# A casting DMA instead of a rounding on ScalarE: the weights' high part straight from DRAM

## The chip, the cores and the metric

The kernel runs on one core of a Trainium2 chip. It is one program for five engines that run side by side and wait for each other by semaphores: TensorE (PE, matrix products), VectorE (DVE), ScalarE (ACT), GpSimd (POOL) and SyncE (SP). DMA transfers are issued by SyncE, GpSimd and ScalarE, each from its own queue in order. The metric is the device time of one execution in microseconds. The median before is 1366.24 us of 3 runs (1365.65 to 1368.66).

## The reference

One layer of a decoder, for a prompt of 1024 tokens and for 8 decode tokens:

```python
h = _rmsnorm(x, norm1_g)
proj = h @ w_in                                   # 1024 x 2304
pool_out = pool_mixer(proj[..., :512])            # windows 2, 4, 8, 16
rwkv_out = rwkv7_mixer(proj[..., 512:])           # 8 heads of 64, state update
x = x + concat(pool_out, rwkv_out) @ w_out        # 1024 x 1024
h2 = _rmsnorm(x, norm2_g)
x = x + square(relu(h2 @ w_up)) @ w_down          # 1024 x 4096, 4096 x 1024
y = _rmsnorm(x, norm_f_g)
```

All inputs are float32. The large products (w_in, w_out, w_up, w_down) are computed in three parts: a float32 operand is split into a high part, rounded to the format fp32r, and a low part, the rest of the subtraction. High times high, high times low and low times high are added up in PSUM.

## The kernel before

The tokens stand in columns, 1032 of them, and a product is computed in blocks of up to 512 columns: blocks of 256 (one of 264) for w_in, and the three blocks BLK of 512, 260 and 260 columns in the MLP. A weight tile `[P, 512]` holds four 128 x 128 weights. For w_in and w_up a row of outputs takes two tiles, for w_down one (four of the 32 hidden tiles at a time).

`weights(src)` brings a tile. It loads the raw float32 tile `wr` (4 buffers, NWR) by a DMA of GpSimd's queue (line 155 or 157), ScalarE rounds it into the high part `wh` (by `act`, line 92; the call is on line 164), and VectorE subtracts to get the low part `wl` (line 165). `wh` and `wl` have 6 buffers each (NWH). So a raw tile waits for the subtract of the tile four back, a high part for the last matmul that reads the tile six back. `gemm` issues the matmuls (line 175), three for each weight, the one with the low weight last.

The stages: at the start the tokens are loaded and split (`token_block`); then the mixer, twice, once for each half of the prompt (`ORDER` gives the sequence of its steps). `R` steps are projections, `S` and `I` prepare a unit of two heads (the inverse of its triangular blocks goes through DRAM: `blk<-AA` on line 464, `Dg<-blk` on line 467, and then line 512, all on SyncE's queue), and `C` is the chain over time. The output projection follows, first for 512 columns, then, with `opb`, for 520. Then the MLP: 32 up tiles `ups_of(f)` (their PSUM pool has four buffers), and eight groups of eight down tiles `down(g, m, b, w)`. In groups 0 to 6 the order is four ups, eight downs. A down block goes into the PSUM pool `psd`, which has two buffers, and VectorE adds it to the residual `x` (line 949); these lines of `down` and its loop are not in the listing below:

```python
ps_d = open_pool(ctx, "psd", 2, space=PSUM)
def down(g, m, b, w):
    ps = ps_d.tile([P, 512], F32, tag="d", name=f"dn{g}_{m}_{b}")
    gemm(ps[:, :n], w, [...])
    V.tensor_tensor(d, ps[:, :n], d, op=ALU.add)
for m in range(KT):
    w = weights(I["w_down"][g, m])
    for b in range(3):
        down(g, m, b, w)
```

The order of each engine's instructions is set when the program is built, by a scheduler that goes by priorities (in the order of the code, moved by `tc.high_priority`) and its own costs. On the chip each engine works through its queue in that order: an instruction that waits holds up those behind it.

Of the kernel before, what the change touches and what calls it, by code (L numbers as in the profile page):

```python
# [15 lines left out]
P = 128  # L16
# [68 lines left out]
def _build(ctx, nc, tc, I, O, dbg):  # L85
    V, A, PE, SY, GP = nc.vector, nc.scalar, nc.tensor, nc.sync, nc.gpsimd

    def f32(ap):
        return ap.bitcast(F32)

    def act(out, in_, func=AF.Copy, bias=0.0, scale=1.0, **k):
        A.activation(out, in_, func, bias=bias, scale=scale, **k)  # L92
# [54 lines left out]
    def weights(src, into=None):  # L147

        out = []
        n = int(np.prod(src.shape[1:]))  # L150
        for o in range(0, n, 512):
            w = min(512, n - o)
            raw = wp.tile([P, 512], F32, tag="wr", name="wr", bufs=NWR)
            if len(src.shape) > 2:
                GP.dma_start(raw.rearrange("p (m c) -> p m c", c=P), src)
            else:
                GP.dma_start(raw[:, :w], src[:, o:o + w])
            if into:
                h, l = into
            else:  # L160
                h = wp.tile([P, 512], F32R, tag="wh", name="wh", bufs=NWH)
                l = wp.tile([P, 512], F32R, tag="wl", name="wl", bufs=NWH)
            with tc.high_priority(offset=LEADW):
                act(h[:, :w], raw[:, :w])
                V.tensor_tensor(l[:, :w], raw[:, :w], f32(h[:, :w]), op=ALU.subtract)  # L165
            out += [(h[:, c:c + P], l[:, c:c + P]) for c in range(0, w, P)]
        return out
# [96 lines left out]
    def project(m, half, use):  # L264
        w = ahead.pop(m, None) or weights(I["w_in"][m])
        for b in (2 * half, 2 * half + 1):
            if b in late:
                with tc.high_priority(offset=LEADX):
                    next(late.pop(b))
            project_block(m, w, b, use)  # L270
# [442 lines left out]
    def pool_group(g, half):  # L713
# [8 lines left out]
        def use(b, n, ps, rs):  # L722
            l0 = 16 + 256 * (b % 2)
            V.tensor_tensor(u[:, l0:l0 + n], ps[:, :n], rs[:, :n], op=ALU.mult)

        w = weights(I["w_in"][g])
        for i in range(2):
            project_block(g, w, 2 * half + i, use)
# [45 lines left out]

    starts = [token_block(b) for b in range(2)]
    ahead[16] = weights(I["w_in"][16, :, 0:512])
    next(starts[0])
    ahead[16] += weights(I["w_in"][16, :, 512:])
# [7 lines left out]
    for w, r, src in ((wup, R[0], "w_lora_up"), (aup, R[1], "a_lora_up")):  # L786
        raw = wp.tile([P, 512], F32, tag="wr", name=f"r{src}", bufs=NWR)
# [128 lines left out]
    with tc.tile_pool(name="opb", bufs=1, reuse_waits="tile") as op:  # L916
        ops = [mixed(op, k, 1, 3) for k in range(KT - 1)]
        for m in range(KT):
            w = weights(I["w_out"][m, :, :(KT - 1) * P])
# [12 lines left out]
    w = weights(I["w_up"][0])  # L932
# [20 lines left out]
    for g in range(7):  # L953
        ups_of(4 * g + 4)
        for m in range(KT):
            w = weights(I["w_down"][g, m])
# [111 lines left out]
```

## Time and profile before

| | before |
|---|---|
| median of 3 runs | 1366.24 us |
| profiled execution | 1369.13 us |
| its span | 1367.4 us |
| TensorE busy | 1306.5 us (96%) |
| VectorE busy | 829.6 us (61%) |
| ScalarE busy | 592.7 us (43%), of these 143.8 in 230 roundings of 512 columns |
| GpSimd busy | 156.5 us (11%) |
| DMA traffic | 94.82 MB, 66.04 of them by GpSimd's queue |
| mean granted TensorE clock | 0.987 |

The span is the time from the first to the last instruction. Matmuls are pipelined and their ends are modelled, so two matmuls overlap in the trace, and TensorE's busy time is not the time that it needs. A wait is put down to what came last. The chain of work that ended last is followed back from the last instruction: at each step to what released it, or to the instruction before it on its engine.

### The profile page before, as it was taken

The numbers are of one execution on the slowest core, as the hardware profiler recorded it, in microseconds if no ns is written. First come the engines' busy times: TensorE is split into PE (matmuls) and PEld (weight loads), VectorE is DVE, ScalarE is ACT, GpSimd is POOL, SyncE is SP. The second block draws the span as 40 slices with busy tenths as digits, with TensorE's granted clock in tenths as the row PEclk, the third lists the DMA queues.
The fourth block names the chain that finished last, engine by engine and source line by source line (L and its number), as shares of the span: only waits on it lengthen the run. The fifth ranks groups of instructions, "written<-read, shape, count | busy, mean of one in ns | idle before, by whom it ended". The sixth has DMA issues, their size and how long they took to land.

```text
span 1367.4 us, 24591 instructions
## 1 busy us (share of the span) xinstructions
PE 1306.5 (96%) x9844; PEld 1158.8 (85%) x9844; DVE 829.6 (61%) x1832; ACT 592.7 (43%) x1466; POOL 156.5 (11%) x306
## 2 busy tenths in 40 slices
PE   5999999999999999999999999999999999999996
PEld 5987778788777777798999999999999999999986
DVE  8887677778778656748644435445444354453447
ACT  7768777877777758526211212112111121121123
POOL 4101000210010021120010100100000100000000
PEclk9999999899999989999999999999999999999998
DMA  6323123222221244531111111111111111111103
GB/s 199 97 55 89 39 47 83 100 96 54 59 63 42 67 152 147 167 125 59 47 54 39 55 47 39 55 40 47 55 40 54 47 46 48 45 48 48 47 7 124
DMA packets 75315, 94.82 MB, mean 69 GB/s; under 512 B 46168, under 2 KB 52440, under 8 KB 75192
## 3 DMA queue, kind: packets, MB, share of 16 engines
q0 software_dynamic: 20480, 66.04, 15.1%
q1 hardware_dynamic: 53392, 25.36, 7.1%
q10 hardware_dynamic: 1328, 1.85, 0.4%
q8 instruction: 77, 1.26, 0.4%
q14 instruction: 38, 0.31, 0.1%
HBM read 79.67 MB, written 13.78 MB: 68 GB/s over the span
## 4 chain that ended last, share of the span: by engine, by line
PE 75%; ACT 9%; DVE 9%; DMA 3%; issue 2%; POOL 1%; SPq 0%; DVEq 0%; POOLq 0%; ACTq 0%
PE dn L175 26%; PE up L175 26%; PE pj L175 7%; PE mx L175 5%; ACT SV L92 2%; DVE tm L496 1%; PE sc L403 1%; PE pcs L580 1%; ACT Es L92 1%; ACT TT L92 1%; PE pcs L577 1%; DVE SV L589 1%; ACT wh L92 1%; PE pcs L573 1%; PE bkt L417 1%
## 5 line engine op out<-in xcount | busy, mean ns | idle before, releaser
L92 ACT ACTIVATE wh<-wr 128x512 fp32r<-128x512 f32 x230 | 143.8, 626 | 353.4 <-PE dn L175 276.2
L175 PE MATMUL up<-h2h,wl 128*128 128x260 f32 (+1 forms) x768 | 245.8, 320 | 0.0
L175 PE MATMUL up<-h2h,wh 128*128 128x260 f32 (+1 forms) x768 | 245.2, 320 | 0.5 <-DVE u L910 0.5
L175 PE MATMUL up<-h2l,wh 128*128 128x260 f32 (+1 forms) x768 | 245.0, 320 | 0.0
L175 PE MATMUL dn<-uh,wl 128*128 128x512 f32 (+1 forms) x720 | 231.2, 321 | 0.0
L175 PE MATMUL dn<-ul,wh 128*128 128x512 f32 (+1 forms) x720 | 230.8, 321 | 0.0
L175 PE MATMUL dn<-uh,wh 128*128 128x512 f32 (+1 forms) x720 | 230.5, 320 | 0.0
L949 DVE TENSOR_TENSOR x<-dn,x 128x260 f32<-128x260 f32 (+1 forms) x192 | 99.1, 516 | 189.8 <-PE dn L175 189.8
L175 PE MATMUL pj<-xh,wh 128*128 128x256 f32 (+1 forms) x576 | 175.3, 304 | 13.9 <-ACT wh L92 13.7
L165 DVE TENSOR_TENSOR wl<-wr,wh 128x512 fp32r<-128x512 f32 x230 | 156.5, 684 | 44.6 <-ACT wh L92 37.8
L175 PE MATMUL pj<-xh,wl 128*128 128x256 f32 (+1 forms) x576 | 171.0, 297 | 0.2 <-DVE wl L165 0.2
L175 PE MATMUL pj<-xl,wh 128*128 128x256 f32 (+1 forms) x576 | 170.5, 296 | 0.0
L175 PEld LDWEIGHTS up<-h2l,wh 128*128 128x128 f32 x768 | 144.6, 188 | 12.1 <-DVE h2l L892 0.4
L175 PEld LDWEIGHTS up<-h2h,wh 128*128 128x128 f32 x768 | 144.3, 188 | 11.6 <-DVE u L910 0.9
L175 PEld LDWEIGHTS up<-h2h,wl 128*128 128x128 f32 x768 | 144.6, 188 | 11.0
L92 ACT ACTIVATE uh<-u 128x260 fp32r<-128x260 f32 (+1 forms) x96 | 47.2, 492 | 238.6 <-DVE u L911 238.6
L175 PEld LDWEIGHTS dn<-ul,wh 128*128 128x128 f32 x720 | 135.6, 188 | 10.9 <-issue 0.2
L175 PEld LDWEIGHTS dn<-uh,wh 128*128 128x128 f32 x720 | 135.8, 189 | 10.4
L175 PEld LDWEIGHTS dn<-uh,wl 128*128 128x128 f32 x720 | 135.5, 188 | 10.6 <-issue 0.2
L175 PEld LDWEIGHTS pj<-xh,wh 128*128 128x128 f32 x576 | 111.4, 193 | 17.4 <-ACT wh L92 13.7
L910 DVE SCALAR_TENSOR_TENSOR u<-up,rs 128x260 f32<-128x260 f32 (+1 forms) x96 | 49.5, 517 | 120.9 <-PE up L175 114.3
L175 PEld LDWEIGHTS pj<-xl,wh 128*128 128x128 f32 x576 | 111.2, 193 | 2.4 <-issue 1.9
(295 smaller groups left out, 2224.3 us busy)
## 6 DMA issues: line engine op xcount, KB each, us to landing
wr<-in_w_in POOLq DMA_DIRECT2D x72, 256.0 KB, 3.1
wr<-in_w_up POOLq DMA_DIRECT2D x64, 256.0 KB, 2.8
wr<-in_w_down POOLq DMA_DIRECT2D x64, 256.0 KB, 2.9
wr<-in_w_out POOLq DMA_DIRECT2D x26, 256.0 KB, 3.1
xr<-in_xT SPq DMA_DIRECT2D x16, 256.0 KB, 3.7
mr<-mix SPq DMA_DIRECT2D x8, 260.0 KB, 3.5
x<-in_xT SPq DMA_DIRECT2D x2, 1040.0 KB, 9.1
blk<-AA SPq DMA_DIRECT2D x16, 128.0 KB, 3.3
```

The source lines that it names most:

```text
L92: A.activation(out, in_, func, bias=bias, scale=scale, **k)
L165: V.tensor_tensor(l[:, :w], raw[:, :w], f32(h[:, :w]), op=ALU.subtract)
L175: PE.matmul(ps, lhs, rhs, start=i == 0, stop=i == n - 1)
L403: PE.matmul(psc[:, c, :], BK[:, c, 2 * h:2 * h + 2, :], AR[:, c, :, h, :], start=True, stop=True)
L417: PE.transpose(pt[:, c, :], BK[:, c, 2 * h:2 * h + 2, :].rearrange("p a t -> p (a t)"), ident)
L496: V.tensor_tensor(pr[:, q], l[:, q].unsqueeze(2).to_broadcast([64, m, m, m]), r[:, q].rearrange("p k j -> p j k").unsqueeze(1).to_broadcas ...
L573: PE.matmul(pq, AR[:, c, 0, :, :], SV[:, c, :, :], start=True, stop=True)
L577: PE.matmul(pa, TT[:, g, :, :], Q, start=True, stop=True)
L580: PE.matmul(pu, BKT[:, c, :, :], SV[:, c, :, :], start=True, stop=True)
L589: V.scalar_tensor_tensor(dst, pu[R[h], h, :], U.gam[R[h], g:g + 1], sg[R[h], h, :], ALU.mult, ALU.add)
L910: V.scalar_tensor_tensor(u, ps[:, :n], 0.0, rs2[:, cs], ALU.max, ALU.mult)
L949: V.tensor_tensor(d, ps[:, :n], d, op=ALU.add)
```

## The change

The high part is no longer rounded by ScalarE. The same piece of DRAM is loaded twice: by SyncE's queue into the raw tile, and by GpSimd's queue into the high part's tile, whose type is fp32r, so that this transfer converts. The subtract stays. The whole diff:

```diff
             raw = wp.tile([P, 512], F32, tag="wr", name="wr", bufs=NWR)
-            if len(src.shape) > 2:
-                GP.dma_start(raw.rearrange("p (m c) -> p m c", c=P), src)
-            else:
-                GP.dma_start(raw[:, :w], src[:, o:o + w])
             if into:
                 h, l = into
             else:
                 h = wp.tile([P, 512], F32R, tag="wh", name="wh", bufs=NWH)
                 l = wp.tile([P, 512], F32R, tag="wl", name="wl", bufs=NWH)
+            for q, t in ((SY, raw), (GP, h)):
+                if len(src.shape) > 2:
+                    q.dma_start(t.rearrange("p (m c) -> p m c", c=P), src)
+                else:
+                    q.dma_start(t[:, :w], src[:, o:o + w])
             with tc.high_priority(offset=LEADW):
-                act(h[:, :w], raw[:, :w])
                 V.tensor_tensor(l[:, :w], raw[:, :w], f32(h[:, :w]), op=ALU.subtract)
```

In the rows below the names are those of the program with a running number; a name in brackets is an engine or a DMA queue whose semaphore the instruction waits for (DMASW is GpSimd's queue, DMAHW SyncE's).

VectorE in the down loop, group 1, from the last block of tile 0 to the first of tile 2, before (`dn1_0_2` is group 1, tile 0, block 2; `wl_9514` belongs to tile 6):

```order
L949 TENSOR_TENSOR x11_7127<-dn1_0_2_9257,x11_7127 128x260 [waits PE_49]
L165 TENSOR_TENSOR wl_9514<-wr_9511,wh_9513 128x512 [waits DMASW1_49,Activation_49]
L949 TENSOR_TENSOR x10_6590<-dn1_1_0_9277,x10_6590 128x512 [waits PE_49]
L949 TENSOR_TENSOR x11_7127<-dn1_1_1_9291,x11_7127 128x260 [waits PE_49]
L949 TENSOR_TENSOR x11_7127<-dn1_1_2_9305,x11_7127 128x260 [waits PE_49]
L165 TENSOR_TENSOR wl_9562<-wr_9559,wh_9561 128x512 [waits DMASW2_49,Activation_49]
L949 TENSOR_TENSOR x10_6590<-dn1_2_0_9325,x10_6590 128x512 [waits PE_49]
```

And after the change:

```order
L949 TENSOR_TENSOR x11_7127<-dn1_0_2_9257,x11_7127 128x260 [waits PE_49]
L165 TENSOR_TENSOR wl_9513<-wr_9511,wh_9512 128x512 [waits DMAHW6_49,DMASW1_49]
L949 TENSOR_TENSOR x10_6590<-dn1_1_0_9277,x10_6590 128x512 [waits PE_49]
L949 TENSOR_TENSOR x11_7127<-dn1_1_1_9291,x11_7127 128x260 [waits PE_49]
L949 TENSOR_TENSOR x11_7127<-dn1_1_2_9305,x11_7127 128x260 [waits PE_49]
L165 TENSOR_TENSOR wl_9561<-wr_9559,wh_9560 128x512 [waits DMAHW7_49,DMASW2_49]
L949 TENSOR_TENSOR x10_6590<-dn1_2_0_9325,x10_6590 128x512 [waits PE_49]
```

Nothing has moved there, but the subtract waits for two transfers where it waited for ScalarE. In groups 0 to 6 a subtract stands right before the evacuation of a down block 56 times.

GpSimd's queue, the down tiles 2 to 6 of the same group, before:

```order
L157 DMA wr_9319<-in_w_down 128x512 [waits DMASW1_49,DVE_49]
L157 DMA wr_9367<-in_w_down 128x512 [waits DMASW2_49,DVE_49]
L157 DMA wr_9415<-in_w_down 128x512 [waits DMASW3_49,DVE_49]
L157 DMA wr_9463<-in_w_down 128x512 [waits DMASW4_49,DVE_49]
L157 DMA wr_9511<-in_w_down 128x512 [waits DMASW5_49,DVE_49]
```

And after:

```order
L163 DMA wh_9320<-in_w_down 128x512 [waits DMASW7_49,DVE_49,PE_49]
L163 DMA wh_9368<-in_w_down 128x512 [waits DMASW0_49,DVE_49,PE_49]
L163 DMA wh_9416<-in_w_down 128x512 [waits DMASW1_49,DVE_49,PE_49]
L163 DMA wh_9464<-in_w_down 128x512 [waits DMASW2_49,DVE_49,PE_49]
L163 DMA wh_9512<-in_w_down 128x512 [waits DMASW3_49,DVE_49,PE_49]
```

A load that waited for VectorE's subtract of the tile four back now waits for TensorE's matmuls with the tile six back.

SyncE's queue in the mixer, around the block inverse of unit 0 (`AA`, `blk`, `Dg`), before:

```order
L707 DMA sp_1307<-in_state_poolT 128x480 [waits DMAHW2_49,Activation_49]
L464 DMA blk0_160<-AA0_0_679 64x8x64 [waits DMAHW3_49,Activation_49]
L464 DMA blk0_160<-AA0_0_679 64x8x64 [waits DMAHW4_49,Activation_49]
L467 DMA Dg0_0_1030<-blk0_160 32x16x16 [waits DMAHW5_49,DMAHW4_49,DMAHW3_49]
L467 DMA Dg0_0_1030<-blk0_160 32x16x16 [waits DMAHW6_49]
```

And after:

```order
L163 DMA wr_1526<-in_w_in 128x512 [waits DMAHW1_49,DVE_49]
L163 DMA wr_1532<-in_w_in 128x512 [waits DMAHW2_49,DVE_49]
L464 DMA blk0_160<-AA0_0_679 64x8x64 [waits Activation_49] x2
L163 DMA wr_1599<-in_w_in 128x512 [waits DMAHW3_49,DVE_49]
L163 DMA wr_1605<-in_w_in 128x512 [waits DMAHW4_49,DVE_49]
L163 DMA wr_2088<-in_w_in 128x512 [waits DMAHW5_49,DVE_49]
L467 DMA Dg0_0_1030<-blk0_160 32x16x16 [waits DMAHW7_49,DMAHW0_49]
L467 DMA Dg0_0_1030<-blk0_160 32x16x16
```

The raw loads, which were in GpSimd's queue, stand between the store of a unit's blocks and their read-back.

## Rows read from the trace of the kernel before

**Rows 1.** The page, part 4: the chain that ended last, by engine, by line.
```profile
PE 75%; ACT 9%; DVE 9%; DMA 3%; issue 2%; POOL 1%; SPq 0%; DVEq 0%; POOLq 0%; ACTq 0%
PE dn L175 26%; PE up L175 26%; PE pj L175 7%; PE mx L175 5%; ACT SV L92 2%; DVE tm L496 1%; PE sc L403 1%; PE pcs L580 1%; ACT Es L92 1%; ACT TT L92 1%; PE pcs L577 1%; DVE SV L589 1%; ACT wh L92 1%; PE pcs L573 1%; PE bkt L417 1%
```
**Rows 2.** Busy time by stage; the columns are named in the first row.
```profile
core 0: us, PE busy (x) PEld busy (x) DVE busy (x) ACT busy (x) POOL busy (x), PEclk, DMA share, GB/s
60.00:285.00 225.00, 208.45 (x2100) 180.42 (x2099) 173.25 (x435) 169.10 (x466) 25.67 (x57) 0.98 0.26 69
285.00:490.00 205.00, 189.95 (x1940) 164.26 (x1941) 156.95 (x407) 151.42 (x422) 24.31 (x48) 0.99 0.27 72
...
690.00:1310.00 620.00, 620.00 (x3939) 562.07 (x3939) 282.94 (x520) 110.32 (x193) 58.05 (x108) 1.00 0.15 47
```
**Rows 3.** The chain in order of time: start us, us, what.
```profile
684.45 45.24 PE dn L175 x288
729.69 45.20 PE up L175 x288
```
**Rows 4.** Waits from 690 to 1300: us in total, times, longest us.
```profile
ACT wh L92 <- PE dn L175: 276.2, 56, 5.1
```
**Rows 5.** The tile wh from 30 to 500: durations in ns, and waits.
```profile
L92 ACT ACTIVATE wh<-wr x73: 612/630/636, 30.5 to 483.5; 128x512 fp32r<-128x512 f32 x73
...
  PE pj L175: 14.0, 23
```
**Rows 6.** The first rounding and the first matmul: start us, us, instruction, idle time before.
```profile
13.02 1.27 ACT L92 ACTIVATE wh<-wr 128x512 fp32r<-128x512 f32 x2 [2.32 <-DMA wr<-in_w_in]
...
13.71 0.58 PE L175 MATMUL pj<-xh,wh 128*128 128x256 f32 x1 [13.71 <-ACT wh L92]
```
**Rows 7.** TensorE in the down loop, in order of time (group 3, tiles 0, 1).
```profile
961.48 0.28 PE L175 MATMUL dn<-ul,wh 128*128 128x260 f32 x1
...
965.94 0.28 PE L175 MATMUL dn<-uh,wh 128*128 128x260 f32 x1
```
**Rows 8.** ScalarE at the same place.
```profile
961.85 0.63 ACT L92 ACTIVATE wh<-wr 128x512 fp32r<-128x512 f32 x1 [4.24 <-PE dn L175]
```
**Rows 9.** VectorE at the same place.
```profile
957.07 0.68 DVE L165 TENSOR_TENSOR wl<-wr,wh 128x512 fp32r<-128x512 f32 x1
957.67 0.42 DVE L913 TENSOR_TENSOR ul<-u,uh 128x260 fp32r<-128x260 f32 x1
...
962.52 0.69 DVE L165 TENSOR_TENSOR wl<-wr,wh 128x512 fp32r<-128x512 f32 x1 [0.17 <-ACT wh L92]
964.69 0.69 DVE L949 TENSOR_TENSOR x<-dn,x 128x512 f32<-128x512 f32 x1 [1.48 <-PE dn L175]
```
**Rows 10.** GpSimd at the same place.
```profile
963.50 0.54 POOL L157 DMA_DIRECT2D wr<-in_w_up  x1 [4.92 <-DVE wl L165]
```
**Rows 11.** GpSimd's loads of line 157 from 956 to 1046.
```profile
DMA to landing us min/median/max: 2.7/2.9/3.7
```
**Rows 12.** A matmul that waited for an evacuation, in order of time.
```profile
646.76 0.43 DVE L910 SCALAR_TENSOR_TENSOR u<-up,rs 128x260 f32<-128x260 f32 x1 [0.80 <-PE ss L885]
...
647.25 0.39 PE L175 MATMUL up<-h2h,wh 128*128 128x260 f32 x1 [0.52 <-DVE u L910]
```
**Rows 13.** DMA issues of the whole span: count, KB each, median us to landing.
```profile
wr<-in_w_in POOLq DMA_DIRECT2D x72, 256.0 KB, 3.1
...
xr<-in_xT SPq DMA_DIRECT2D x16, 256.0 KB, 3.7
...
pw<-in_pool_w POOLq DMA_DIRECT2D x8, 64.0 KB, 2.4
```
**Rows 14.** SyncE's first loads, in order of time.
```profile
1.19 4.00 SPq L213 DMA_DIRECT2D xr<-in_xT  x8
```
**Rows 15.** The chain in order of time, the first block inverse.
```profile
70.74 4.54 DMA blk<-AA
```

## The prediction

> **What bounds the kernel now.** I read the chain of work that ended last first. TensorE carries 75% of it, the MLP's two lines alone 26% each, ScalarE and VectorE 9% each [rows 1]. The stage table splits the span: from 690 to 1310 us (the MLP) TensorE is busy in all 620 us, ScalarE in 110 and VectorE in 283; in the two mixer stages (60 to 490) VectorE and ScalarE are both busy for about three quarters of the time, and TensorE is not always [rows 2]. So the MLP is paced by TensorE with nothing to spare for it, and the mixer is a braid of three engines. In the MLP the reader should see how regular it is: a group of eight down tiles takes 45.2 us, so one tile (twelve matmuls for each of three blocks of 512, 260 and 260 columns) 5.66 us, and four up tiles take as long [rows 3].
>
> The rounding is where the next weight tile meets the work. A tile's high part can only be written when one of six buffers is free, that is when TensorE has done with the tile six back. In the MLP ScalarE waited for that 56 times, 276.2 us in all [rows 4]: once for each of the 56 down tiles of groups 0 to 6. It costs nothing, as ScalarE has nothing else to do there. After the change this wait stands in GpSimd's queue, and a DMA follows it instead of a 0.63 us ACTIVATE.
>
> **What the change removes.** 234 roundings on ScalarE at 0.63 us, 147 us of its time. In the MLP they are beside TensorE's work, worth nothing. In the mixer there are 73, 46 us [rows 5]; the chain itself holds 1% of the span in them, some 14 us [rows 1]. At the start TensorE waited for the first rounding, 13.02 to 13.71 [rows 6]: 0.7 us saved.
>
> **What it adds: the landing, on VectorE's path.** VectorE's order in the down loop is the same before and after: evacuate the last block of tile m, subtract for tile m+6, evacuate the first block of tile m+1. But the subtract now waits for a transfer that is issued only when tile m's matmuls are over. Behind it in VectorE's queue stands the evacuation of the next 512-column block, and for that waits TensorE: the pool of down blocks has two buffers, so the third block of tile m+1 needs the buffer of its first.
>
> Worked out for one tile. The last matmul that reads the high part starts at 961.48, and ScalarE begins the rounding that waited for it at 961.85 [rows 7, 8]. GpSimd starts a load 0.29 us after what releases it (the subtract of 962.52 ends at 963.21, the load starts at 963.50) [rows 9, 10]: 962.14. Loads in these loops land 2.9 us after their issue (2.7 to 3.7) [rows 11]: 965.04. The next VectorE instruction starts 0.60 us after a subtract starts (957.07 to 957.67), the evacuation takes 0.69 [rows 9]: it ends at 966.33 instead of 965.38. TensorE goes on 0.06 us after the evacuation that it waited for (646.76 and 0.43, then 647.25) [rows 12]: 966.39. In the trace of before the third block began at 965.94 [rows 7]. So each tile loses 0.45 us, and as the next release is counted from the delayed block, the loss repeats: 56 × 0.45 = 25.2 us. Each 0.1 us of landing is worth 5.6 us from a landing of 2.45 us on.
>
> The landing of a transfer that converts is not in the trace, so it is bounded by its neighbours: from below by GpSimd's 64 KB load at 2.4 us (no loss at all), from above by the slowest load of these loops, 3.7, which is also SyncE's median beside other traffic [rows 11, 13] (1.25 us a tile, 70 us). I take 2.9, the row with the same bytes, queue and stage.
>
> Of the Trainium skill, one page bears on this: "DMA: Bandwidth & Descriptors", section "Anatomy of one DMA — SWDGE (gpsimd) path". It says that a semaphore wait is served on the issuing sequencer before dispatch, the DMA engines never wait; that speaks against this change, since a load that waits for TensorE cannot be under way early, and the late start of GpSimd's loads agrees [rows 10]. By the page's fit, 2.0 us and the bytes by 436 GB/s, 256 KB would land after an estimated 2.6 us and the loop would lose 0.15 × 56 = 8 us; the trace's 2.9 decides. No page prices the conversion, and no run here shows it yet.
>
> **The other places.** The up loop is covered: its two subtracts come after the last block of a tile, the second would end about 0.29 + 0.54 + 2.9 + 2 × 0.69 = 5.1 us after the release even if both loads started only then, and the next up block of 512 columns takes TensorE 45.20 / 4 × 512 / 1032 = 5.6 us [rows 3, 9, 10]. The pool has four buffers there besides. If that cover went, each late 0.1 us would cost 2 to 3 us over 28 tiles. The 34 output-projection tiles I count at nothing: there the subtracts stand after both blocks of a tile, and TensorE's next need is a whole tile away; at most 34 × 0.45 = 15 us.
>
> In the mixer the same wait falls on VectorE. ScalarE had to wait for a free buffer 23 times of 73 [rows 5]; those tiles now come 0.29 + 3.1 − 0.63, some 2.7 us later than a rounding would give them, up to 63 us of VectorE standing. VectorE's part of the chain is 9% of the span, 123 us, nearly all within the first 690, so about 18%: 11 us on the path. Bounds for the stage: 46 us gained (every rounding was in the way) to 63 lost (every wait is). I take 14 gained and 11 lost. The raw loads move into SyncE's queue, where they stand among the transfers of the block inverse; three come between the store and the read-back of unit 0, at 0.5 us an issue [rows 14], and that store is on the chain [rows 15]: 1.5 us lost. The weights' traffic doubles, from 47 to some 94 GB/s in the MLP, where the DMA engines are 15% busy [rows 2]: hidden.
>
> **Sum,** against the profiled execution's 1369.13 us (span 1367.4, 1.7 around it): + 25.2 − 0.7 − 14 + 11 + 1.5 = + 23 us, 1392. That execution was 2.9 us over the median of the three timed runs (1366.24), so the prediction is 1366.2 + 23, about 1390 us.
>
> **Rivals.** (1) The converting transfer lands late. For it: nothing in this kernel converts in a DMA, so no row rules it out; against it: 256 KB is little, and the DMA engines are idle most of the time. Every microsecond beyond 2.9 is 56 us more in the down loop: at 3.7, 1366 + 23 + 45 = 1434; at 4.2, 1462. (2) ScalarE was the mixer's bound. It is busy 169 of 225 and 151 of 205 us [rows 2], its queue is in order, and a rounding that waits for TensorE holds up everything behind it; without 73 of them the stage could shorten by up to 46 us. It decides when the relief exceeds the down loop's loss by more than the rest, that is from about 30 us on; with all of it and no VectorE waits, 1366 + 25 + 1.5 − 46.7 = 1346. Against it: the chain holds only 14 us in roundings, and VectorE is as full as ScalarE. (3) The wait is hidden after all: the landing is at most 2.45 us, as for the 64 KB load, or TensorE's release comes earlier than I read it, and the mixer's gain and loss cancel: 1366.
>
> **Chances.** Forecast 57%, by itself 1372 to 1425 (landing 2.7 to 3.3, the mixer 15 us either way); late landing 20%, all slower; mixer relief 16%, faster; hidden 7%, no change. 0.2% (2.7 us) is about what a measurement of this kernel can tell from none. So faster 16%, same 7%, slower 77%. The range of 1362 to 1440 leaves out most of the relief case and the upper third of the late landings.
>
> **What will show it.** Right: in the chain of the MLP, VectorE's subtracts and evacuations and GpSimd's loads between runs of down matmuls; VectorE waiting for the DMA of the high part about 56 times in the down loop, TensorE for VectorE's evacuation; eight down tiles taking 48.9 us (45.2 and 8 × 0.45), four up tiles still 45.2. Wrong: down groups of 45.2 us (the landing is hidden), or up groups that grow too (the weights come too late, not only VectorE). A stretch from 60 to 490 us that is shorter or longer by over 15 us would mean that I misread the mixer. The landing of the loads of the high part against 2.9 us tells which of the cases it is.

## The result and the profile after

The changed kernel takes 1416.85 us (median of 4 runs, 1413.67 to 1423.02), the kernel before 1365.95 (4 runs). The ratio is 1.0376, interval 1.0354 to 1.0398: 51 us slower, where 24 were forecast. The profiled execution took 1423.02 us (span 1421.3), 53.9 more than the one of before.

Three marks in TensorE's timeline split these 53.9 us. The first matmul of down group 0 starts at 699.59 us, before at 684.28: 15.3 us are lost before it. The seven down groups that alternate with ups take 355.5 us, before 317.5: 37.9. The up groups between them take 45.2 us as before; one that begins at the low clock takes 0.9 more. The end is as long as before, 60 us.

The page of the changed kernel, its first line of busy times and the chain by engine and by line, beside [rows 1]:

```profile
PE 1327.2 (93%) x9844; PEld 1164.3 (82%) x9844; DVE 822.1 (58%) x1832; ACT 455.9 (32%) x1232; POOL 155.2 (11%) x306
...
issue 50%; PE 13%; POOL 5%; DMA 4%; DVE 4%; ACT 4%; POOLq 0%; SPq 0%; DVEq 0%; ACTq 0%
POOL wh L163 5%; PE dn L175 3%; PE up L175 2%; PE mx L175 1%; DMA wh<-in_w_out 1%; PE pj L175 1%; DMA wh<-in_w_in 1%; ACT SV L92 1%; PE pcs L580 1%; ACT Es L92 1%; DMA mr<-mix 1%; DMA x<-in_xT 1%; DMA wh<-in_w_up 0%; DVE wl L165 0%; PE pcs L577 0%
```

ScalarE is 137 us less busy and nothing is faster. The chain is no longer TensorE's: in the MLP it runs back through GpSimd's loads, one behind the other, with "issue" between them. That is a chain that follows GpSimd's own queue and puts GpSimd's waiting down as issue; how long TensorE stood has to be read from the waits and the timeline.

The waits of the MLP (690 to 1360 us: total, times, longest), where [rows 4] had ScalarE waiting 276.2 us without harm:

```profile
POOL wh L163 <- PE dn L175: 317.7, 55, 8.2
...
DVE wl L165 <- DMA wh<-in_w_up: 125.0, 54, 5.1
...
DVE wl L165 <- DMA wh<-in_w_down: 66.5, 56, 3.8
...
PEld dn L175 <- DVE x L949: 31.6, 54, 2.9
```

The wait has moved to GpSimd, and VectorE and TensorE now wait behind it. One down tile in order of time, first TensorE, then GpSimd, then VectorE (start us, us, instruction, idle time before it):

```profile
717.72 0.28 PE L175 MATMUL dn<-ul,wh 128*128 128x260 f32 x1
...
722.06 0.28 PE L175 MATMUL dn<-uh,wl 128*128 128x260 f32 x1
722.61 0.39 PE L175 MATMUL dn<-uh,wh 128*128 128x260 f32 x1 [0.27 <-DVE x L949]
```
```profile
718.30 0.53 POOL L163 DMA_DIRECT2D wh<-in_w_up  x1 [5.65 <-PE dn L175]
```
```profile
718.16 0.43 DVE L949 TENSOR_TENSOR x<-dn,x 128x260 f32<-128x260 f32 x1 [1.47 <-PE dn L175]
721.27 0.69 DVE L165 TENSOR_TENSOR wl<-wr,wh 128x512 fp32r<-128x512 f32 x1 [2.68 <-DMA wh<-in_w_up]
721.88 1.02 DVE L949 TENSOR_TENSOR x<-dn,x 128x512 f32<-128x512 f32 x2
```

The load starts 0.3 us after the last matmul that reads the old high part has ended (718.00), the subtract starts 2.97 us later, the evacuation of the 512 columns 0.61 us after that, and TensorE's third block waits for it. Over the 56 loads of these loops the subtract starts 2.76 to 4.73 us after its load, median 2.90, and where the clock is full and GpSimd is not late the time from one release to the next is this lag plus 3.23 us, almost to 0.01: 2.76 gives 5.99, 2.90 gives 6.13, 4.13 gives 7.36. A tile of 5.66 us [rows 3] stands for a lag of 2.43; above that, every tenth is paid in full.

A few late loads make a quarter of the down loop's loss. GpSimd's loads in the MLP, issue to landing, in the changed kernel and in the kernel before:

```profile
DMA to landing us min/median/max: 2.7/2.9/4.7
```
```profile
DMA to landing us min/median/max: 2.7/2.8/3.8
```

Five of the 56 subtracts started 3.9 to 4.7 us after their load, and one load started 2.4 us late. That one, on GpSimd, VectorE and TensorE:

```profile
1032.36 0.53 POOL L163 DMA_DIRECT2D wh<-in_w_up  x1 [7.98 <-issue]
```
```profile
1035.29 0.69 DVE L165 TENSOR_TENSOR wl<-wr,wh 128x512 fp32r<-128x512 f32 x1 [5.11 <-DMA wh<-in_w_up]
```
```profile
1033.66 0.28 PE L175 MATMUL dn<-uh,wl 128*128 128x260 f32 x1
1036.64 0.39 PE L175 MATMUL dn<-uh,wh 128*128 128x260 f32 x1 [2.69 <-DVE x L949]
...
1038.80 0.63 PE L175 MATMUL up<-h2h,wh 128*128 128x512 f32 x1
...
1041.11 0.39 PE L175 MATMUL up<-h2h,wh 128*128 128x512 f32 x1
```

TensorE stood 2.69 us, and soon after it ran at the lower of its two levels: a matmul of 512 columns takes 0.63 us instead of 0.39. The granted clock of a stretch that holds both levels (columns as in [rows 2]):

```profile
1036.00:1040.50 4.50, 3.86 (x16) 3.49 (x17) 1.35 (x3) 0.00 (x0) 0.53 (x1) 0.66 0.24 63
```

It is 1.00 again from 1041 to 1045 us. So this stall is paid a second time, in part, by the clock. The late start itself is not new: in the kernel before GpSimd has it too, at its load of 977.27 us, 8.12 us after the load before it where its neighbours are 5.6 us apart, and nothing waits for it there:

```profile
977.27 0.54 POOL L157 DMA_DIRECT2D wr<-in_w_up  x1 [7.58 <-DVE x L949]
```

In both kernels it is the 216th DMA that GpSimd issues.

The stages (stretch, us, busy time of PE, PEld, DVE, ACT, POOL, clock, DMA share, GB/s), the mixer beside [rows 2]:

```profile
60.00:285.00 225.00, 209.19 (x2108) 180.51 (x2107) 175.39 (x438) 153.48 (x437) 26.35 (x58) 0.98 0.39 103
285.00:490.00 205.00, 186.37 (x1815) 160.91 (x1813) 155.25 (x402) 129.64 (x381) 23.35 (x46) 0.99 0.40 104
```

The stages are the same with less ScalarE work; the last projection's matmul is at 483.75 us (483.28 before). The 15 us show only after it. The stretch 484 to 700, before and after:

```profile
484.00:700.00 216.00, 208.53 (x1447) 179.12 (x1446) 137.26 (x282) 107.44 (x273) 31.91 (x59) 0.97 0.33 108
```
```profile
484.00:700.00 216.00, 198.07 (x1353) 168.38 (x1352) 130.70 (x271) 82.15 (x225) 29.93 (x56) 0.94 0.53 160
```

The granted clock is 0.94 instead of 0.97 here, by the rounded figures some 6 us of full speed (0.03 × 216). VectorE in that stretch, after the change, where the output projection's first tiles meet the last steps of the chain over time (`SV`, line 589):

```profile
518.37 0.57 DVE L589 SCALAR_TENSOR_TENSOR SV<-pcs,gam,sg 64x64 f32<-64x64 f32 x2
...
519.08 0.68 DVE L673 TENSOR_TENSOR dS<-dS,dT 128x512 f32<-128x512 f32 x1
523.42 0.69 DVE L165 TENSOR_TENSOR wl<-wr,wh 128x512 fp32r<-128x512 f32 x1 [3.66 <-DMA wh<-in_w_out]
...
525.22 0.57 DVE L589 SCALAR_TENSOR_TENSOR SV<-pcs,gam,sg 64x64 f32<-64x64 f32 x2
```

VectorE stands 3.66 us at the subtract of a w_out tile, and the next chain step is behind it. The last chain step on TensorE is at 542.67 us, before at 530.55. VectorE's waits for casting transfers from 0 to 640 us (total, times, longest):

```profile
DVE wl L165 <- DMA wh<-in_w_out: 30.2, 15, 3.9
DVE wl L165 <- DMA wh<-in_w_in: 19.8, 16, 3.0
```

The 15.3 us have a second part. The MLP's first matmul (up tile 0) is at 631.12 us, before at 619.61: 11.5 us. From there to group 0 TensorE does five up tiles and the last of the output projection in 68.5 us, before 64.7: 3.8 us more, at a granted clock of 0.98, before 1.00. VectorE stands at subtracts of w_up here, and behind them are evacuations and the sums of squares of the norm, for which TensorE waits. VectorE and TensorE after, TensorE before:

```profile
633.04 0.69 DVE L165 TENSOR_TENSOR wl<-wr,wh 128x512 fp32r<-128x512 f32 x1 [1.28 <-DMA wh<-in_w_up]
656.18 0.69 DVE L165 TENSOR_TENSOR wl<-wr,wh 128x512 fp32r<-128x512 f32 x1 [0.71 <-DMA wh<-in_w_up]
```
```profile
634.12 0.39 PE L175 MATMUL mx<-mh,wh 128*128 128x260 f32 x1 [0.95 <-DVE x L860]
659.94 0.49 PE L885 MATMUL ss<-acc,cst 128*128 128x260 f32 x1 [2.04 <-DVE acc L883]
```
```profile
646.02 0.49 PE L885 MATMUL ss<-acc,cst 128*128 128x260 f32 x1 [0.74 <-DVE acc L883]
```

### The profile page after: what moved, and what is told of

It reads as the page before. It is cut to its first block, busy times and chain, and to the rows that moved or that the text cites. A ratio compares the mean times of both kernels' runs of the same rounds, so it can differ in the third digit from the quotient of the medians.

```text
span 1421.3 us, 24704 instructions
## 1 busy us (share of the span) xinstructions
PE 1327.2 (93%) x9844; PEld 1164.3 (82%) x9844; DVE 822.1 (58%) x1832; ACT 455.9 (32%) x1232; POOL 155.2 (11%) x306
## 4 chain that ended last, share of the span: by engine, by line
issue 50%; PE 13%; POOL 5%; DMA 4%; DVE 4%; ACT 4%; POOLq 0%; SPq 0%; DVEq 0%; ACTq 0%
POOL wh L163 5%; PE dn L175 3%; PE up L175 2%; PE mx L175 1%; DMA wh<-in_w_out 1%; PE pj L175 1%; DMA wh<-in_w_in 1%; ACT SV L92 1%; PE pcs L580 1%; ACT Es L92 1%; DMA mr<-mix 1%; DMA x<-in_xT 1%; DMA wh<-in_w_up 0%; DVE wl L165 0%; PE pcs L577 0%
## 5 line engine op out<-in xcount | busy, mean ns | idle before, releaser
L175 PE MATMUL dn<-uh,wh 128*128 128x512 f32 (+1 forms) x720 | 237.7, 330 | 20.4 <-DVE x L949 18.6
L949 DVE TENSOR_TENSOR x<-dn,x 128x260 f32<-128x260 f32 (+1 forms) x192 | 94.7, 512 | 91.4 <-PE dn L175 91.3
L175 PEld LDWEIGHTS pj<-xh,wl 128*128 128x128 f32 x576 | 109.8, 191 | 2.0 <-issue 1.2
```

What stands on the lines that cost most here:

```text
L175: PE.matmul(ps, lhs, rhs, start=i == 0, stop=i == n - 1)
```

## The experiments

Every kernel was timed beside the kernel before, both on the same chip. The last two columns are from its profiled execution: the start of down group 0, and the mean of the seven down groups.

| kernel | median us | ratio to before (95%) | group 0 at | down group |
|---|---|---|---|---|
| before | 1366 | | 684.3 | 45.4 |
| the change | 1416.9 | 1.0376 (1.0354 to 1.0398) | 699.6 | 50.8 |
| 1: 7 high, 5 low parts | 1368.9 | 1.0017 (0.9999 to 1.0035) | 684.1 | 45.4 |
| 2: four PSUM buffers | 1383.6 | 1.0124 (1.0095 to 1.0153) | 697.2 | 45.4 |
| 3: w_up, w_down alone | 1403.4 | 1.0266 (1.0241 to 1.0292) | 684.6 | 50.1 |
| 4: w_in, w_out alone | 1376.8 | 1.0075 (1.0054 to 1.0097) | 690.2 | 45.4 |
| 5: w_down alone | 1379.5 | 1.0095 (1.0079 to 1.0111) | 681.2 | 47.3 |
| 6: w_out alone | 1379.5 | 1.0085 (1.0058 to 1.0112) | 695.2 | 45.4 |
| 7: w_in alone | 1374.0 | 1.0060 (1.0040 to 1.0080) | 686.9 | 45.4 |
| 8: stores by SyncE | 1422.6 | 1.0410 (1.0391 to 1.0429) | 699.8 | 50.8 |
| 9: loads in halves | 1387.2 | 1.0148 (1.0124 to 1.0172) | 699.3 | 45.8 |
| 10: raw loads moved alone | 1365.6 | 0.9993 (0.9977 to 1.0009) | 680.6 | 45.4 |
| 11: before, with 7 and 5 | 1369.1 | 1.0022 (1.0003 to 1.0040) | 680.8 | 45.4 |
| 12: w_in alone, 7 and 5 | 1367.4 | 1.0009 (0.9990 to 1.0028) | 681.1 | 45.4 |
| 13: no wait, all weights | 1366.1 | 0.9996 (0.9987 to 1.0006) | 682.5 | 45.4 |
| 14: no wait, w_in, w_out | 1407.6 | 1.0298 (1.0276 to 1.0320) | 687.5 | 50.3 |

Theory A: VectorE stands at a subtract until the transfer has landed, and what stands behind it in its queue decides what that costs. Rival B: TensorE, or a queue, waits for the weights themselves.

**1. One high part more, one low part less.**

```diff
-                h = wp.tile([P, 512], F32R, tag="wh", name="wh", bufs=NWH)
-                l = wp.tile([P, 512], F32R, tag="wl", name="wl", bufs=NWH)
+                h = wp.tile([P, 512], F32R, tag="wh", name="wh", bufs=7)
+                l = wp.tile([P, 512], F32R, tag="wl", name="wl", bufs=5)
```

> One buffer goes from the low parts to the high parts (7 and 5 instead of 6 and 6); everything else is the changed kernel. VectorE's order in the down loop keeps the same pattern (a subtract right before the first evacuation of a down tile), but a high part's load is released two tiles (11 us) before its subtract stands there. Theory A (VectorE stands at the subtract until the transfer has landed, and TensorE waits for the evacuation behind it): the down groups fall from 49.0 to 52.0 us back to 45.2 to 45.6, the late landings of 4 to 5 us are covered too, the low clock after them goes; the MLP gets some 38 us back: 1372 to 1385 us, if five low parts cost the mixer nothing. Rival B (the doubled traffic makes every load of the MLP late, or TensorE itself waits for weights): down groups stay at 49 us or more, 1410 to 1420.

48 of the 51 us are gone, more than A expected of the MLP: the loss before it has gone too, and with it VectorE's waits there (4.2 us from 0 to 640, at w_in alone). The chain of waits from 640 us on has its old form:

```profile
684.27 45.24 PE dn L175 x288
729.51 45.20 PE up L175 x288
```

GpSimd waits as long as ever for TensorE (578 us from 640 to 1365), but two tiles ahead of the subtract. VectorE waits there for a casting transfer only twice, 2.1 us in all, in the last down group, where no ups alternate any more. As many bytes are moved by the same queues, so traffic and SyncE's queue are not the cause.

**2. Two PSUM buffers more for the down blocks.**

```diff
-        ps = ps_d.tile([P, 512], F32, tag="d", name=f"dn{g}_{m}_{b}")
+        pool, tag = ((ps_d, "d"), (ps_m, "m"))[(m * 3 + b) % 2]
+        ps = pool.tile([P, 512], F32, tag=tag, name=f"dn{g}_{m}_{b}")
```

> The changed kernel, but the blocks of the down loop go in turn into two PSUM pools of two buffers each (four in place of two); loads, subtracts and VectorE's order stay. Theory A: VectorE still stands at each subtract until the transfer has landed (about 55 waits on the load of the high part), but TensorE no longer needs the block that stands behind it: down groups 45.2 to 45.6 us where the landing is 2.9 us, a late landing of 4.7 us covered as well; 1372 to 1385 us. Rival B (TensorE waits for the weights, not for the evacuation): no change, down groups 49 us or more, 1410 to 1420.

1383.6, as A has it. The waits from 640 to 1365 us still show VectorE standing:

```profile
DVE wl L165 <- DMA wh<-in_w_up: 120.1, 54, 5.1
...
DVE wl L165 <- DMA wh<-in_w_down: 66.1, 57, 2.8
```

and the down groups are those of before. VectorE's wait alone costs nothing there; it costs where TensorE needs the evacuation behind it.

**3 and 4. The change for some of the weights.** `cast=True` at the calls for w_up and w_down (3), for w_in and w_out (4):

```diff
-            for q, t in ((SY, raw), (GP, h)):
+            for q, t in ((SY, raw), (GP, h)) if cast else ((GP, raw),):
...
+                if not cast:
+                    act(h[:, :w], raw[:, :w])
```

> The change for w_up and w_down alone; w_in and w_out are rounded by ScalarE as before. If the trace is read rightly, the MLP loses the same 36 to 40 us (down groups 49 to 52 us, up groups 45.2) and all before it is as before (the first down group begins at 684 us): 1400 to 1408 us. Rival: the losses before the MLP are not from the mixer's weights (the raw loads of the MLP in SyncE's queue, say): the first down group begins late, near 699 us, and the time is that of the whole change, 1413 to 1420.

> The change for w_in and w_out alone; w_up and w_down are rounded by ScalarE as before. Theory: the loss of some 15 us before the MLP is all here and the MLP is as before (down groups 45.2 us): 1376 to 1386 us. Rival (the relief of ScalarE is worth something in the mixer, and the loss comes only together with the MLP's part): 1366 or less.

Both as expected: by the ratios 36 us are lost with the MLP's weights and 10 with the others, together 46 of 51, each known to some 3 us.

**5. The change for w_down alone.** `cast=True` only there.

> The change for w_down alone; all other weights are rounded by ScalarE. In the down loop of a group the subtracts that stand before the evacuations are those of the tiles six ahead: of the last two down tiles in its first two tiles, of up tiles in the other six. Theory A (VectorE's queue is what TensorE waits for, so that it counts which subtracts stand there and not which weights the loop uses): 2 of 8 tiles lose, 14 in all, 14 x 0.43 us and a quarter of the late landings, 6 to 9 us: 1371 to 1376 us; the first two down tiles of a group take 6.1 us, the others 5.66. Rival B (TensorE waits for the down weights themselves): all 56 tiles lose, 1395 to 1405 us.

1379.5, 13 us more than before: B is out by far, but the loss is larger than I expected. The profile shows three tiles of a group that lose, not two: the subtract before the first evacuation of a group also belongs to a down tile. Two subtracts of group 1, the last one that waits for a transfer and the first that waits for ScalarE:

```profile
788.88 0.69 DVE L167 TENSOR_TENSOR wl<-wr,wh 128x512 fp32r<-128x512 f32 x1 [2.56 <-DMA wh<-in_w_down]
792.54 0.69 DVE L167 TENSOR_TENSOR wl<-wr,wh 128x512 fp32r<-128x512 f32 x1 [0.17 <-ACT wh L92]
```

The first three tiles of a group take 6.0 to 6.5 us (two take 7.2 and 8.0), the other five 5.65 to 5.70. 21 tiles by 0.45 and the two late ones make the 13 us.

**6 and 7. w_out alone, w_in alone.**

> The change for w_out alone (34 tiles of the output projection). Theory: the loss before the MLP is VectorE standing at w_out's subtracts among the last steps of the chain over time, about 10 us as with w_in and w_out together: 1374 to 1379 us. Rival (the loss comes from w_in, or from the two together): 1364 to 1369.

> The change for w_in alone (72 tiles of the mixer's projections). Theory: relief of ScalarE and waits of VectorE cancel, as the last projection ends at 483 us before and after: 1364 to 1370 us. Rival (w_in makes the loss before the MLP): 1374 to 1379; rival (the relief shows once w_out's loss is gone): under 1363.

w_out is as expected, half a microsecond over the range. w_in is not: 8 us slower, neither the cancelling nor the relief, and at the lower end of the rival by which w_in makes the loss. In its trace the last projection is where it was (483.5 us), but the last chain step is at 537 us, before at 531, with no casting tile of w_out there. VectorE's waits for w_in are 17.4 us from 0 to 545; the way from them to that step was not followed. Apart they lose 11.6 and 8.2, together (run 4) 10.2: the losses do not add up.

**8. The stores off GpSimd's queue.** `QUEUE = 2` instead of 1.

> The changed kernel with the stores of the mixers' results and outputs moved from GpSimd's queue to SyncE's, so that no store stands behind a load that waits for a free high part. Theory (VectorE's waits at w_out's subtracts make the loss before the MLP): no gain beyond 3 us, the first down group begins at 695 to 702 us, 1412 to 1420 us. Rival (the stores held up in GpSimd's queue make it): the first down group begins near 686 us and the time is 1400 to 1407.

No gain (the time is a little above the range, its interval overlaps with the whole change's): stores held up behind a load on GpSimd are not the loss.

**9. The MLP's high parts in two halves.**

```diff
+                elif halves and q is GP:
+                    q.dma_start(t[:, :256], src[:, o:o + 256])
+                    q.dma_start(t[:, 256:w], src[:, o + 256:o + w])
```

> The changed kernel, but the MLP's high parts are loaded in two halves of 256 columns each. GpSimd issues twice per tile (0.5 us more), so the landing is not earlier; and the scheduler, which reckons with a later landing, now puts each subtract of the down loop behind the evacuation of the next tile's 512 columns instead of before it. Theory A (what stands behind the waiting subtract decides): TensorE gets its buffer in time, the next evacuation behind the subtract has some 2 us to spare, down groups 45.2 to 46 us; the loss before the MLP stays: 1376 to 1388 us. Rival B (the landing itself is what TensorE waits for): with 0.3 to 0.5 us more of landing the 56 tiles lose 17 to 28 us more, 1432 to 1446 us.

A's range. The halves land 2.4 us after their issue (median), the second issued 0.5 us later, so the tile is no earlier than in one piece. But the subtract now stands behind the urgent evacuation:

```profile
713.61 0.69 DVE L952 TENSOR_TENSOR x<-dn,x 128x512 f32<-128x512 f32 x1 [2.34 <-PE dn L178]
714.22 0.68 DVE L168 TENSOR_TENSOR wl<-wr,wh 128x512 fp32r<-128x512 f32 x1
```

And 41 of the 49 tile times that lie inside groups are those of before (5.65 to 5.70 us). Of the other eight two stand out (6.5 and 6.9 us); the second follows GpSimd's 216th issue, which is late here too.

**10. The raw loads by SyncE alone.** Raw tiles by SyncE's queue, rounding on ScalarE, one load a tile.

> Only the raw loads move to SyncE's queue; the high part is rounded by ScalarE as before and nothing is loaded twice. Theory (the queue's part of the change is small): down groups 45.2 us, the first down group within 3 us of 684 us: 1364 to 1371 us. Rival (the raw loads among the transfers of the block inverse and the mixers' stores make the loss before the MLP): 1374 to 1382.

No difference in time, but not because nothing moved. SyncE issues the first weight load at 1.20 us, where GpSimd's queue has it behind fills until 7.09, and the first matmul starts at 5.78 instead of 13.71 [rows 6]:

```profile
5.78 0.58 PE L176 MATMUL pj<-xh,wh 128*128 128x256 f32 x1 [5.78 <-ACT xh L92]
```

From there to the last projection it takes 470.2 us, before 469.6: so far the queue costs next to nothing. The 7.4 us that are left of the early start are halved by group 0 (680.6 instead of 684.3) and not to be seen in the time. From the last projection to group 0 the kernel before and runs 1, 3, 5, 11, 12 and 13 need 199 to 205 us, this one 204.6; so no run tells whether the queue takes back what the start gained. The whole change has no early start (13.62), as its first high part still comes by GpSimd.

**11 and 12. Controls with seven and five buffers.** The kernel before, and the change for w_in alone.

> The kernel before with seven high parts and five low parts instead of six and six: the control for the run with seven and five. Theory (buffers matter only where a load follows the release; a rounding of 0.63 us is hidden with six): 1362 to 1370 us. Rival (the split of buffers is itself a gain, which would hide a loss of the casting transfers): under 1360.

> The change for w_in alone, with seven high parts and five low parts; all other weights are rounded by ScalarE. Theory (with a load released a tile earlier the mixer keeps ScalarE's relief without VectorE's waits; the last projection ended 3 us earlier in the whole change with these buffers): 1360 to 1367 us. Rival (the relief is off the path): 1366 to 1372.

Buffers alone give nothing. In run 12 the 8 us of run 7 are gone and with them most of VectorE's waits for w_in (4.5 us from 0 to 545 instead of 17.4); but the time is the rival's: ScalarE's relief in the mixer is worth nothing that can be measured.

**13 and 14. VectorE's wait taken away, the transfers left.** For all weights (13), for w_in and w_out (14). The low parts are then zero, so these kernels leave the products with the low weights out of the result; instructions and transfers are as many as before the edit:

```diff
-                V.tensor_tensor(l[:, :w], raw[:, :w], f32(h[:, :w]), op=ALU.subtract)
+                V.tensor_tensor(l[:, :w], raw[:, :w], raw[:, :w], op=ALU.subtract)
```

> The changed kernel, but every low part is the raw tile less itself (zero, so the low weights are left out of the products): the subtract needs the raw tile alone, and VectorE never waits for a casting transfer; transfers, buffers and matmuls are as many as in the changed kernel, and TensorE still needs the high parts that the casting transfers bring. Theory A (the whole loss, before the MLP and in it, is VectorE standing at the subtracts): down groups 45.2 to 45.7 us, the first down group within 4 us of 684 us, 1362 to 1373 us. Rival (TensorE or a queue waits for the high parts themselves): the first down group stays near 697 us, or the down groups near 50; 1378 or more.

> The same for w_in and w_out alone (their low parts are zero and left out); the MLP's subtracts wait as in the changed kernel. Theory (the loss of 15 us before the MLP is VectorE standing at the subtracts of w_in and w_out): the first down group within 4 us of 684 us and 1398 to 1408 us, the time of the change for w_up and w_down alone. Rival (GpSimd's queue, or TensorE waiting for late high parts): the first down group at 694 to 700 us, 1411 to 1420 us.

These settle the cause. With the same transfers, buffers and matmuls, and VectorE waiting for the raw tile only, run 13 takes the time of the kernel before. Its chain from 640 us on:

```profile
682.67 45.24 PE dn L175 x288
727.91 45.20 PE up L175 x288
```

One of its transfers in the MLP took 6.2 us to land, and TensorE did not stop. In run 14 group 0 starts at 687.5 instead of 699.6: of the 15 us before the MLP, some 12 are VectorE standing at the subtracts of w_in and w_out. The other 3 lie in the stretch from up tile 0 to group 0. Up tile 0 starts at 618.1 us in run 14 and 617.4 in run 13, before at 619.6 and with the whole change at 631.1. From there to group 0 the kernels that round w_up with six buffers take 64.7 us, runs 1 and 13, where nothing waits for w_up's transfers, 65.1, and the changed kernel and runs 2, 3, 8, 9 and 14, where VectorE does, 67.1 to 70.3 (68.4 in run 3, 69.5 in run 14). Seven and five buffers with w_up rounded (11 and 12) take 66.4, so not all of such a difference needs a casting transfer. Of the 4 us from run 3 to run 14, 2.9 are there by group 0 and 1.2 come in the down groups. No version beats the kernel before by more than can be measured.

## Why the prediction was too low

The direction and the mechanism were right; the size was not, 24 us for 51. By the steps:

**The landing on VectorE's path: right.** 0.45 us a tile and 25.2 us in all were forecast. The median tile takes 6.13 us instead of 5.66: 0.47 × 56 = 26 us. The point from which it counts, 2.45 us, is 2.43 in the trace, from the load's start to the subtract's. That these agree so well is luck in part: the sum counted GpSimd's 0.29 us from ScalarE's start, 0.09 us after the matmul had ended, and left out that the subtract starts 0.02 to 0.09 us after the landing. In the MLP a transfer that converts lands at most 0.1 us later than a plain one (2.9 and 2.8 us): that unknown, on which the first rival rested, was chosen rightly. The Trainium skill ("DMA: Bandwidth & Descriptors", "Anatomy of one DMA — SWDGE (gpsimd) path") says that a semaphore wait is served on the issuing sequencer before dispatch; the load's start 0.3 us after TensorE's release agrees. Its fit gave an estimated 2.6 us; 2.9 is measured, and the measurement decides.

**"I take 2.9": the term that was mis-sized.** The loop lost 37.9 us, not 25.2. I multiplied a median by 56. But the loss is linear in the landing once it is over the threshold, so the mean counts, and the late ones count in full: four late landings inside the loops are together 6.5 us over the median, the late load 2.4, and the lower clock after three long stalls most of the 3 us that are left. The row that I quoted had its maximum of 3.7 in it [rows 11], and I used that as a bound for all tiles instead of a price for some.

**"The 34 output-projection tiles I count at nothing": failed.** I looked at the second half's tiles, whose subtracts follow both blocks, and found a whole tile of cover. The first half's tiles lie among the last steps of the chain over time, and there the same wait holds up `SV` on VectorE: the last chain step is at 540 us with w_out alone (run 6), at 528 and 529 without the waits (runs 13 and 14), before at 531. Run 6 puts 11.6 us on w_out, and runs 4 and 14 put 10 to 12 on w_in and w_out together, close to the upper bound of 15 that I had named and not taken.

**"The up loop is covered": right for the up groups, wrong at the start of the MLP.** The six groups between down loops take 45.2 us as before. The five tiles before group 0 stand among the output projection's last evacuations and the second norm, and there the waits of w_up cost 3.8 us.

**The mixer: its sum near to the last projection, wrong to the end.** −0.7, −14, + 11 and + 1.5 made −2; the last projection ends 0.5 us later than before. Without VectorE's waits it ends at 477.6 us (run 13), so relief and waits are some 6 us each to that point, not 14 and 11; that they cancel so well there is luck in the terms. The relief does not outlast it: run 13 as a whole is no faster. The waits do: w_in alone is 8.2 us slower (run 7), where the sum has −2, and 1.2, within the noise, with most of its waits taken away (run 12); through which steps they reach the end is open. SyncE's queue costs 0.6 us to the last projection (run 10), where I took 1.5, and the first matmul starts at 13.62 instead of 13.71, where I took 0.7 us off.

**The rivals.** Late landing: not as a rule, but for one load in ten. ScalarE's relief as the winner: refuted by runs 12 and 13. Hidden: refuted. The forecast's own span does not come from its terms at the lower end: a landing of 2.7 and a mixer 15 us better give about 1364, not 1372.

## What to carry to other kernels

A load into a buffer that TensorE must release first cannot start early: replacing an engine's copy into such a buffer by a DMA turns a copy's 0.6 us after the release into a landing of 2.9, unless one more buffer lets it start a tile earlier. What a wait costs is read from what stands behind it in its engine's queue, at every place where that instruction occurs and not at the most regular one: two PSUM buffers more, one high part more or another order each took the down loop's loss away (45.4, 45.4 and 45.8 us a group instead of 50.8). Where a transfer's landing is on the path, sum its mean with its late cases, not its median.

## What had not been expected of the hardware

In the MLP the conversion adds at most 0.1 us to a load's landing (2.9 us for 256 KB on GpSimd's queue, 2.8 without it). For w_out the landing was 3.7 us instead of 3.1, but 3.1 with the same conversion in run 13, so this is not the conversion alone. About one such load in ten lands 1 to 2 us later than the rest, in a loop where the DMA engines are a third busy; what delays them is not shown by any run. The one late start is no such chance: in each of the kernels whose raw or high parts come by GpSimd, the one before included, GpSimd's 216th DMA (in run 8, without its stores, the 214th) starts some 2 to 2.5 us late, whatever the tile and the time (822 us in run 9, 1032 in the changed kernel). Why it is this one is not shown. Two halves of 128 KB land 2.4 us after their issues, so splitting gains 0.5 us a piece, which the second issue costs again.
